# RWKV r, v and output weights split layers ahead and kept in DRAM, r and v in three products, bonus product on Pool

## The chip, the cores and the metric

One core of a Trainium2 chip runs the whole kernel. The metric is the device time in microseconds. The engines are TensorE (PE), VectorE (DVE), ScalarE (ACT), GpSimd (Pool) and SyncE (SP); SP issues nearly all DMAs. The 16 DMA engines of the core are shared by every transfer. On-chip memory is SBUF, and DRAM is the chip's own off-chip memory.

## The reference, cut to what matters

Two layers, SEQ = 256 tokens of D = 1024, float32. Layer 0 mixes by a gated MLP, layer 1 by RWKV-7; each layer has a SwiGLU FFN before and after the mixer and a gated embedding (ple) at its end.

```python
for i in range(DEPTH):                       # DEPTH = 2
    h = h + 0.5 * rms_norm(swiglu(rms_norm(h, g[0]), ffn_w13[i, 0], ffn_w2[i, 0]), g[1])
    m = gmlp_mixer(...) if i % 2 == 0 else rwkv7_mixer(...)
    h = h + rms_norm(m, g[3])
    h = h + 0.5 * rms_norm(swiglu(rms_norm(h, g[4]), ffn_w13[i, 1], ffn_w2[i, 1]), g[5])
    ...                                      # ple

# in rwkv7_mixer: H = 16 heads of N = 64
x_rkv = h[:, :, None, :] + dx[:, :, None, :] * mu[:3]
rkv = jnp.einsum('bsnd,nde->bsne', x_rkv, w_in)      # w_in[0], [1], [2]: r, k, v, 1024x1024 each
g = jax.nn.sigmoid(xg @ g1) @ g2
k = k * (1.0 + (a - 1.0) * k_a)
y = wkv7_scan(rh, heads(decay), kh, vh, -kk, kk * ah)
bonus = (jnp.sum(rh * kh * r_k, axis=-1, keepdims=True) * vh).reshape(B, S, D)
out = ((yn + bonus) * g) @ w_out                     # w_out: 1024x1024
```

## The kernel before, in words

The stages run in the order ffn00, gmlp, ffn01, ple0, ffn10, rwkv, ffn11, ple1, with seams in which the work of two neighbours is mixed. The Tile framework fixes the order of instructions on every engine when the program is built; an engine runs its own list strictly in order and waits on semaphores.

**Weights.** They come as units of 128x1024 float32 (512 KB). `emit_dma` has SP load a unit into one of 4 raw buffers (L134). `emit_split` casts it to fp32r on ACT, the high half (L154), and subtracts on DVE, the low half (L156); both halves go into one slot of 128x2048 (1 MB). There are 20 slots, handed out in a ring by `slot` and `drop`; weights and the activations of a stage share them. Four raw loads are issued ahead of the split, and `pump` splits at most 12 units ahead of their use. `mm3` multiplies split values in three fp32r products (L178 to L180). The FFN works by 11 chunks of 256 of the 2816 hidden columns: AT(c) multiplies by w13 (L400, which packs the products by one half), copies the result out (L408, ACT) and makes the gate; Dn(c) multiplies by w2 (L178 to L180).

**RWKV weights.** The k weights are split as usual. r (L1055) and v (L1307) are not: their "wf" loads of 1 MB (L146, two row blocks each) go into a slot, and both are multiplied in plain float32. The output weights (o) are split inside the stage, as slots come free.

**RWKV order.** `xprod(n)` makes the mixed input of projection n on DVE (L819). After k come the eight `r_step`s, among which `triangle` (L1039) makes the matrices that the scan inverts. A ladder of small DVE products and sums (L1091, L1093) then inverts the 16x16 diagonal blocks, and two transposes (L1094, L1095) hand the inverse to PE. While DVE climbs it, PE does `gate1` (L1171), the eight `v_step`s and `gate2` (L1198, L1203). `join(0)` (L1110) and `join(1)` (L1121) lie between the products of v_step(5) and v_step(6) and need the ladder's result. `inside(k)` (L1284, L1292) makes the scores of head pair k. Among the ladder DVE has eight products of r with the decay (L1268) and the bonus product kT*rT (L1269). Then `stack_v` (L1389) fills the state operands, and chunk(0) to chunk(3) run the recurrence, each as us (L1415), a copy (L1444), st (L1453) and y. `spread` (L1493) and `scaled` (L1504) normalise, `otr` transposes, and Dn(0), Dn(1) multiply by the output weights.

```python
        def r_step(k):
            w = self.need(at["r"] + k // 2)[0][:, k % 2]
            for m in range(KT):
                mm(psr[m // 2][:, (m % 2) * T:(m % 2 + 1) * T], lhsT=w[:, m * 128:(m + 1) * 128], rhs=xent(0, k),
                   start=k == 0 and m % 2 == 0, stop=k == KT - 1 and m % 2 == 1)
```

Of the kernel before, what the change touches and what calls it, by code (L numbers as in the profile page):

```python
# [60 lines left out]
class Trunk:  # L61
    NSLOT = 20

    def __init__(self, ctx, tc, io):
# [4 lines left out]
        ep = lambda name, bufs=1, **k: ctx.enter_context(tc.tile_pool(name=name, bufs=bufs, **k))
        self.slots = ep("slots")  # L70
        self.pp = ep("pp", space=bass.MemoryType.PSUM)
        self.rawp = ep("raw", 4)
# [17 lines left out]
        self.pq = {}  # L90

# [45 lines left out]
    def emit_split(self):  # L137
# [3 lines left out]
        if len(self.units[i]) > 3:  # L141
# [8 lines left out]
        src, p, n = self.units[i]  # L150
# [6 lines left out]
        self.hl[i] = (hl, hh, ll)  # L157
# [148 lines left out]
    def ffn_units(self, f):  # L306
# [468 lines left out]
    def rwkv_units(self):  # L775
# [6 lines left out]
        rows = lambda n: [(io["wrkv"][n, k * 256:(k + 1) * 256, :].rearrange("(k p) d -> p k d", p=128), 128, D, 2) for k in range(KT // 2)]  # L782
        put("k", [(io["wrkv"][1, k * 128:(k + 1) * 128, :], 128, D) for k in range(KT)])
        put("l", [(io["wl"], 128, 1024, 2)])
        put("r", rows(0))
        put("g1", [(io["g1"].rearrange("q p n -> p q n"), 128, 640, 2)])
        put("g2", [(io["g2"], 128, D, 2)])
        put("v", rows(2))
        put("o", [(io["bwout"][k * 128:(k + 1) * 128, :], 128, D) for k in range(KT)])
        return at  # L790

    def rwkv(self, at):
# [20 lines left out]
        def xprod(n, lo=0, hi=T, ks=range(KT)):  # L813
# [135 lines left out]
        xprod(0)  # L949
        wu_ = self.slot("wu")  # L950
# [100 lines left out]
        def r_step(k):  # L1051

            w = self.need(at["r"] + k // 2)[0][:, k % 2]
            for m in range(KT):
                mm(psr[m // 2][:, (m % 2) * T:(m % 2 + 1) * T], lhsT=w[:, m * 128:(m + 1) * 128], rhs=xent(0, k),  # L1055
                   start=k == 0 and m % 2 == 0, stop=k == KT - 1 and m % 2 == 1)
            if k % 2:
                self.release(at["r"] + k // 2)
# [210 lines left out]
        V.tensor_tensor(kT, kT, rT, op=ALU.mult)  # L1269
# [30 lines left out]
        def v_step(k, between=()):  # L1300

            x = xent(2, k)
            w = self.need(at["v"] + k // 2)[0][:, k % 2]
            between = list(between)
            for b in range(NB):
                for q in range(2):
                    mm(psv[b][q], lhsT=x[:, b * 128:(b + 1) * 128], rhs=w[:, q * 512:(q + 1) * 512], start=k == 0, stop=k == KT - 1)  # L1307
                    if between:
                        between.pop(0)()
            if k % 2:  # L1310
                self.release(at["v"] + k // 2)
                if k < 5:
                    P(1, 1)
# [27 lines left out]
        self.drop(X["x"][2])  # L1341
# [34 lines left out]

        sv = [self.slot("sv") for _ in range(2)]
        svv = [t.rearrange("p (c m h t) -> p c m h t", c=2, m=8, h=2) for t in sv]
        vv = vn.rearrange("p (b m h t) -> p b m h t", b=2, m=8, h=2)
        vm = self.small(32, "vm", 1)  # L1380
        vmv = vm.rearrange("p (b m h) -> p b m h", b=2, h=2)
        for b in range(NB):
            V.tensor_reduce(vm[:, b * 16:(b + 1) * 16], vn[:, b * D:(b + 1) * D].rearrange("p (h t) -> p h t", t=64), axis=AX.X, op=ALU.add)
            V.tensor_scalar(vm[:, b * 16:(b + 1) * 16], vm[:, b * 16:(b + 1) * 16], ck[:, 0:1], 1.0 / 64, op0=ALU.mult, op1=ALU.mult)

        def stack_v(c):
            rs = half[c % 2]
            for h in range(2):
                V.scalar_tensor_tensor(svv[c // 2][half[1 - h], c % 2, :, h, :], vv[rs, c // 2, :, h, :], ck[rs, 0:1],  # L1389
                                       vmv[rs, c // 2, :, h].unsqueeze(2).to_broadcast([64, 8, 64]), op0=ALU.mult, op1=ALU.subtract)  # L1390

        for c in range(NCH):
            stack_v(c)
        G.memset(svv[0][EV, 0, :, 0, :], 0.0)
        G.memset(svv[0][OD, 0, :, 1, :], 0.0)
# [284 lines left out]
```

## Time and profile before

| what | value |
|---|---|
| median of 3 runs | 1177.57 us (1177.08 to 1178.36) |
| the profiled execution's own time | 1183.38 us |
| its span | 1181.6 us |
| PE busy | 97% of the span |
| DVE, ACT, Pool busy | 73%, 56%, 6% |
| DMA, mean | 176 GB/s, 207.78 MB |
| ffn01's chunks 2 to 10 | 367.6 to about 510 us of the span |
| rwkv | about 741 to 957 us |

The span is that of the profiler's one execution; about 1.8 us lie around it. A busy PE is not PE at its fastest: the float32 products run longer for the same work, and in a few stretches the granted clock is below full. Times below are microseconds from the span's start.

### The profile page before, as it was taken

The numbers are of one execution on the slowest core, as the hardware profiler recorded it, in microseconds if no ns is written. First come the engines' busy times: TensorE is split into PE (matmuls) and PEld (weight loads), VectorE is DVE, ScalarE is ACT, GpSimd is POOL, SyncE is SP. The second block draws the span as 40 slices with busy tenths as digits, with TensorE's granted clock in tenths as the row PEclk, the third lists the DMA queues.
The fourth block names the chain that finished last, engine by engine and source line by source line (L and its number), as shares of the span: only waits on it lengthen the run. The fifth ranks groups of instructions, "written<-read, shape, count | busy, mean of one in ns | idle before, by whom it ended". The sixth has DMA issues, their size and how long they took to land. (4 is left out here: it accounts for less than half of the span.)

```text
span 1181.6 us, 18709 instructions
## 1 busy us (share of the span) xinstructions
PE 1151.2 (97%) x7284; PEld 954.3 (81%) x7284; DVE 859.1 (73%) x1299; ACT 659.7 (56%) x1145; POOL 72.5 (6%) x92
## 2 busy tenths in 40 slices
PE   8999999999999999999999999999998899999997
PEld 6788888888888888888888888777467778888886
DVE  5886666877678666667876666878859898676663
ACT  6665556545476555558755554374226396555553
POOL 0000000010010000001100000230000220000011
PEclk8999999999999999999999999999989999999999
DMA  7886654746586666646766664550300377666510
GB/s 244 292 295 196 190 172 152 253 156 205 186 271 202 194 192 184 192 134 196 248 189 194 193 192 144 178 183 1 125 4 21 108 249 263 193 189 193 177 47 36
DMA packets 58841, 207.78 MB, mean 176 GB/s; under 512 B 6784, under 2 KB 7296, under 8 KB 58496
## 3 DMA queue, kind: packets, MB, share of 16 engines
q1 hardware_dynamic: 58752, 206.59, 54.8%
q8 instruction: 57, 0.93, 0.3%
q14 instruction: 32, 0.26, 0.1%
HBM read 205.51 MB, written 1.05 MB: 175 GB/s over the span
## 5 line engine op out<-in xcount | busy, mean ns | idle before, releaser
L156 DVE TENSOR_TENSOR w<-raw,w 128x1024 fp32r<-128x1024 f32 x348 | 423.6, 1223 | 145.6 <-ACT w L154 139.8
L154 ACT CAST w<-raw 128x1024 fp32r<-128x1024 f32 x348 | 366.3, 1055 | 153.9 <-PE mm L400 68.7
L400 PE MATMUL mm<-xT,w 128*128 128x512 f32 (+1 forms) x2304 | 407.8, 337 | 0.0
L400 PEld LDWEIGHTS mm<-xT,w 128*128 128x128 f32 x2304 | 358.6, 189 | 50.0
L178 PE MATMUL acc<-w,hT 128*128 128x512 f32 x352 | 138.2, 393 | 0.0
L179 PE MATMUL acc<-w,hT 128*128 128x512 f32 x352 | 137.3, 390 | 0.0
L180 PE MATMUL acc<-w,hT 128*128 128x512 f32 x352 | 137.1, 389 | 0.0
L408 ACT COPY pn<-mm 128x256 f32<-128x256 f32 x144 | 46.6, 375 | 93.8 <-PE mm L400 93.8
L409 DVE TENSOR_TENSOR pn<-mm,pn 128x256 f32<-128x256 f32 x144 | 54.4, 418 | 39.3 <-ACT pn L408 39.3
L180 PEld LDWEIGHTS acc<-w,hT 128*128 128x128 f32 x352 | 66.1, 188 | 14.1
L178 PEld LDWEIGHTS acc<-w,hT 128*128 128x128 f32 x352 | 66.2, 188 | 12.6
L179 PEld LDWEIGHTS acc<-w,hT 128*128 128x128 f32 x352 | 66.3, 188 | 12.3
L232 POOL TENSOR_SCALAR rpost<-ss 128x1 f32<-128x1 f32 x15 | 7.5, 500 | 777.9 <-ACT junk L239 777.9
L178 PE MATMUL mm<-w,xT 128*128 128x512 f32 x128 | 51.8, 415 | 2.9 <-ACT w L154 2.6
L289 DVE SCALAR_TENSOR_TENSOR xT<-tr,gT,xT 128x128 fp32r<-128x128 f32 x112 | 35.6, 344 | 24.4 <-ACT xT L288 23.5
L179 PE MATMUL mm<-w,xT 128*128 128x512 f32 x128 | 51.4, 405 | 0.7 <-DVE xT L289 0.5
L412 DVE TENSOR_TENSOR pn<-pn,yc 128x512 f32<-128x512 f32 x72 | 49.7, 691 | 2.0
L180 PE MATMUL mm<-w,xT 128*128 128x512 f32 x128 | 50.9, 403 | 0.0
L179 PE MATMUL z<-w,xT 128*128 128x512 f32 x128 | 49.9, 390 | 0.0
L180 PE MATMUL z<-w,xT 128*128 128x512 f32 x128 | 49.9, 390 | 0.0
L178 PE MATMUL z<-w,xT 128*128 128x512 f32 x128 | 49.7, 393 | 0.0
L288 ACT ACTIVATE xT<-tr,gT 128x128 fp32r<-128x128 f32 x112 | 37.8, 371 | 19.3 <-PE tr L275 14.9
(282 smaller groups left out, 1534.8 us busy)
## 6 DMA issues: line engine op xcount, KB each, us to landing
raw<-in_w SPq DMA_DIRECT2D x264, 512.0 KB, 4.3
raw<-in_win SPq DMA_DIRECT2D x32, 512.0 KB, 4.4
raw<-in_wout SPq DMA_DIRECT2D x16, 512.0 KB, 4.8
raw<-in_wg SPq DMA_DIRECT2D x16, 512.0 KB, 3.9
wf<-in_wrkv SPq DMA_DIRECT2D x8, 1024.0 KB, 5.1
gbc<-in_norm_g SPq DMA_DIRECT2D x9, 512.0 KB, 5.4
raw<-in_wrkv SPq DMA_DIRECT2D x8, 512.0 KB, 3.5
raw<-in_bwout SPq DMA_DIRECT2D x8, 512.0 KB, 3.6
```

The lines of the kernel that those rows point to most:

```text
L154: self.high = self.nc.scalar.copy(hh, r[:p, :n])
L156: eng.tensor_tensor(ll, r[:p, :n], hh.bitcast(F32), op=ALU.subtract)
L178: mm(out, lhsT=lh, rhs=rh, start=start, stop=False)
L179: mm(out, lhsT=ll, rhs=rh, start=False, stop=False)
L180: mm(out, lhsT=lh, rhs=rl, start=False, stop=stop)
L232: nc.gpsimd.tensor_scalar(r, a, b, eps, op0=ALU.add, op1=ALU.add)
L288: done = (nc.scalar.activation(hi, v, AF.Copy, scale=gc), nc.vector.scalar_tensor_tensor(lo, v, gc, hi.bitcast(F32), op0=ALU.mult, op1=ALU ...
L289: nc.vector.scalar_tensor_tensor(lo, v, gc, hi.bitcast(F32), op0=ALU.mult, op1=ALU.subtract))
L400: nc.tensor.matmul(ps[i][:, :T] if s else ps[i], lhsT=w[:, sl], rhs=x, start=u + q + s == 0, stop=s + u == 2 and q == 3)
L408: nc.scalar.copy(zi, ps[i][:, T:])
L409: nc.vector.tensor_tensor(zi, ps[i][:, :T], zi, op=ALU.add)
L412: nc.vector.tensor_tensor(z2, z2, rbc.unsqueeze(1).to_broadcast([128, 2, T]), op=ALU.mult)
```

## The change

The r and v rows (16 units) join ffn01's list of units, two per chunk from c = 2 to 8 and one in c = 9 and 10; the o rows (8 units) join ffn10's, one per chunk from c = 2 to 9. They are split as every unit is, and `flush` then stores each slot to a DRAM tile (1 MB) and drops it. In the rwkv stage `emit_split` loads that tile (1 MB) into a slot. `parts` splits the inputs of r and v too: ACT casts the high half, and the low half comes from DVE and Pool (r) or Pool twice (v). `r_step` and `v_step` take three fp32r products. `xprod(5)` and `xprod(2)` move ahead of the ladder; kT*rT goes to Pool behind the last low half of v's input; mean and `stack_v` are spread between inside(4) and chunk(1).

```diff
     def emit_split(self):
...
+        self.flush()
+        if len(self.units[i]) > 4:
+
+            t = self.slot("w", F32R)
+            self.nc.sync.dma_start(t.bitcast(F32), self.parts.pop(self.units[i][3]))
+            self.hl[i] = (t, t[:, :1024], t[:, 1024:])
+            self.n_split += 1
+            return
...
+        if len(self.units[i]) > 3:
+
+            self.stores.append((self.units[i][3], hl))
+        else:
+            self.hl[i] = (hl, hh, ll)
...
+    def flush(self):
+        for key, hl in self.stores:
+            t = self.parts[key] = self.rdp.tile([128, 2048], F32, name=f"part_{key}", tag=f"part_{key}")
+            self.nc.sync.dma_start(t, hl.bitcast(F32))
+            self.drop(hl)
+        self.stores.clear()
...
             put(at13, c, w13(c))
             put(at2, c - 2, w2(c - 2))
+            for _ in range(-(-len(early) // (FC - c))):
+                key, src = early.popleft()
+                u.append((src, 128, 1024, key))
...
+        kept = lambda n: [(None, 128, D, f"{n}{k}", True) for k in range(KT)]
...
-        put("r", rows(0))
+        put("r", kept("r"))
...
-        put("v", rows(2))
-        put("o", [(io["bwout"][k * 128:(k + 1) * 128, :], 128, D) for k in range(KT)])
+        put("v", kept("v"))
+        put("o", kept("o"))
...
+        def parts(n, key, engs):
+
+            X[key] = [self.slot("xs", F32R) for _ in range(2)]
+            for i, e in enumerate(engs):
+                ks = slice(i * KT // len(engs), (i + 1) * KT // len(engs))
+                x, xh, xl = (g8(t)[:, ks] for t in (X["x"][n], *X[key]))
+                S.copy(xh, x)
+                L[key] = e.tensor_tensor(xl, x, xh.bitcast(F32), op=ALU.subtract)
+            self.drop(X["x"].pop(n))
...
         xprod(0)
+        parts(0, "r", (V, G))
+        P(1, 8)
...
+                mm(o, lhsT=wh[:, ms], rhs=xh, start=k == 0 and m % 2 == 0, stop=False)
+                mm(o, lhsT=wh[:, ms], rhs=xl, start=False, stop=False)
+                mm(o, lhsT=wl[:, ms], rhs=xh, start=False, stop=k == KT - 1 and m % 2 == 1)
...
+        xprod(5)
         P(1, 3)
-
+        xprod(2)
+        self.drop(hnT, dxT)
+        parts(2, "v", (G, G))
 
         nq = self.slot("nq")
...
-        xprod(5)
         gate1()
-        xprod(2)
-        self.drop(hnT, dxT)
...
-        V.tensor_tensor(kT, kT, rT, op=ALU.mult)
+        with behind("v"):
+            G.tensor_tensor(kT, kT, rT, op=ALU.mult)
...
+                    self.mm3(psv[b][q], xh, xl, wh[:, sl], wl[:, sl], k == 0, k == KT - 1)
...
+        mean_v(0)
+        stack_v(0)
...
         inside(4)
         inside(5)
+        stack_v(1)
...
         chunk(0)
         with behind("c"):
-            P(1, 0)
+            mean_v(1)
+            stack_v(2)
+            P(2, 1)
             vgain(0)
         chunk(1)
         with behind("c"):
-            P(1, 0)
+            stack_v(3)
+            P(2, 1)
             vgain(1)
...
+                    todo = [rows("r", self.io["wrkv"][0]) + rows("v", self.io["wrkv"][2]), rows("o", self.io["bwout"])]
+                    if dist < 2:
+                        early = todo[1 - dist]
+                plan.append(self.ffn_units(st[1] * 2 + st[2], early))
```

The order in which instructions stand shows three places. First SP's own queue in ffn01 (`raw<-in_w` loads an FFN unit, `raw<-in_wrkv` an r or v unit, `part_` is a DRAM tile). Before:

```order
L134 DMA raw<-in_w 128x1024 x18
L222 DMA gbc<-in_norm_g 128x1024
L134 DMA raw<-in_w 128x1024 x48
L134 DMA raw<-in_wp 128x1024 x2
L134 DMA raw<-in_wg 128x1024 x8
```

Of the change, the same place from its first store on:

```order
L181 DMA part_r_3282<-w_3238 128x2048
L138 DMA raw<-in_w 128x1024 x2
L138 DMA raw<-in_wrkv 128x1024 x2
L138 DMA raw<-in_w 128x1024 x3
L181 DMA part_r_3487<-w_3437 128x2048
L138 DMA raw<-in_w 128x1024
L181 DMA part_r_3505<-w_3489 128x2048
L138 DMA raw<-in_w 128x1024 x2
L138 DMA raw<-in_wrkv 128x1024 x2
L138 DMA raw<-in_w 128x1024 x3
```

Two 1 MB stores and two more 512 KB loads now stand among each chunk's loads, and the engines' split instructions with them.

Second, DVE where the ladder begins (`xr` is the mixed input, `wu` the inverse, `mx` the matrices). Before:

```order
L1259 TENSOR_TENSOR q_537_6885<-q_537_6885,kT_6925 128x2048
L1082 MEMSET wu_6881 128x32
L1083 STREAM_TRANSPOSE wu_6881<-mx_6996 128x1024
L1091 TENSOR_TENSOR pn<-wu_6881 128x2
L1093 TENSOR_REDUCE wu_6881<-pn 128x2
L1091 TENSOR_TENSOR pn<-wu_6881 128x8
L819 SCALAR_TENSOR_TENSOR xr_7250<-dxT_6588,chT,hnT_6587 128x256
```

Of the change:

```order
L1049 TENSOR_TENSOR bt_7171<-bt_7171,q_564_7061 128x1024
L846 SCALAR_TENSOR_TENSOR xr_7500<-dxT_6756,chT,hnT_6755 128x256 x7
L1126 MEMSET wu_7057 128x16
L1301 TENSOR_TENSOR q_564_7061<-q_564_7061,kT_7101 128x2048
L1127 MEMSET wu_7057 128x32
L1128 STREAM_TRANSPOSE wu_7057<-mx_7172 128x1024
L846 SCALAR_TENSOR_TENSOR xr_7511<-dxT_6756,chT,hnT_6755 128x256 x8
L1136 TENSOR_TENSOR pn<-wu_7057 128x2
L1138 TENSOR_REDUCE wu_7057<-pn 128x2
```

The eight pieces of xprod(5) moved to the other side of the first transpose, and those of xprod(2) from between the ladder's steps to ahead of them.

Third, Pool at the same place (`nq` is cleared for join(0), `xs` are the halves of v's input). Before:

```order
L904 TENSOR_TENSOR kn_6906<-kn_6906,gn_6907 128x1024
L1078 MEMSET nq_7192 128x2048
L1330 MEMSET xx_7385 32x32x32 x2
L1394 MEMSET sv_8079 64x8x64
L1395 MEMSET sv_8079 64x8x64
```

Of the change:

```order
L941 TENSOR_TENSOR kn_7082<-kn_7082,gn_7083 128x1024
L1123 MEMSET nq_7526 128x2048
L855 TENSOR_TENSOR xs_7521<-xr_7511,xs_7520 128x1024 x2
L1312 TENSOR_TENSOR kT_7101<-kT_7101,rT_7579 128x2048
L1372 MEMSET xx_7736 32x32x32 x2
```

Three products with two inputs each came between the two clears.

## Rows read from the trace of the kernel before

**Rows 1.** The page's head, and its DMA issue line of the unsplit loads.

```profile
span 1181.6 us, 18709 instructions
...
wf<-in_wrkv SPq DMA_DIRECT2D x8, 1024.0 KB, 5.1
```

**Rows 2.** Windows: length, busy time (instructions) of PE, PEld, DVE, ACT, POOL; clock; DMA share; GB/s.

```profile
60.00:80.00 20.00, 20.00 (x108) 17.30 (x107) 16.09 (x23) 13.19 (x20) 1.07 (x1) 1.00 0.91 308
384.60:500.00 115.40, 115.40 (x613) 99.62 (x612) 80.43 (x112) 61.59 (x97) 0.00 (x0) 1.00 0.62 189
820.20:849.10 28.90, 28.88 (x94) 14.56 (x94) 28.58 (x55) 9.38 (x18) 1.89 (x2) 1.00 0.27 92
849.10:871.00 21.90, 19.94 (x595) 11.43 (x597) 6.57 (x8) 0.59 (x1) 0.00 (x0) 0.77 0.16 52
```

**Rows 3.** Waits from 20 to 95 us: total, times, longest.

```profile
ACT w L154 <- DMA raw<-in_w: 16.7, 18, 2.8
```

**Rows 4.** Groups by form, 640 to 960 us: count, busy us, mean ns, idle before.

```profile
L156 DVE TENSOR_TENSOR w<-raw,w 128x1024 fp32r<-128x1024 f32 x48 | 58.2, 1221 | 17.2 <-ACT w L154 16.6
L154 ACT CAST w<-raw 128x1024 fp32r<-128x1024 f32 x48 | 50.4, 1053 | 19.7 <-PE mm L400 11.7 <-PE st L1453 3.0 <-PE acc L180 2.7
```

**Rows 5.** PE's timeline in ffn10: start, duration, engine, operation.

```profile
700.00 11.31 PE L400 MATMUL mm<-xT,w 128*128 128x512 f32 x64
711.15 0.40 PE L178 MATMUL acc<-w,hT 128*128 128x512 f32 x1
...
713.89 0.62 PE L400 MATMUL mm<-xT,w 128*128 128x512 f32 x2
```

**Rows 6.** PE's timeline in the rwkv stage.

```profile
785.54 14.08 PE L1055 MATMUL r<-xr,wf 128*128 128x256 f32 x64
...
820.22 4.58 PE L1171 MATMUL g<-wf,xr 128*128 128x160 f32 x32 [2.37 <-ACT rT L1250]
824.64 3.60 PE L1307 MATMUL v<-wf,xr 128*128 128x512 f32 x8
828.07 0.60 PE L1187 MATMUL g<-ident,gl 128*128 128x128 f32 x4
...
849.14 0.73 PE L1110 MATMUL q<-wu,nq 16*32 16x16 f32 x64
...
859.77 2.07 PE L1307 MATMUL v<-wf,xr 128*128 128x512 f32 x2
861.77 1.05 PE L1121 MATMUL x<-mx,nq 32*32 32x16 f32 x64
...
898.33 0.42 PE L1415 MATMUL us<-sv,sk 128*64 128x64 f32 x4 [2.70 <-DVE sv L1389]
...
904.09 1.15 PE L1453 MATMUL st<-sv,bn 128*64 128x64 f32 x28 [0.71 <-DVE sv L1444]
```

**Rows 7.** DVE's timeline in the rwkv stage.

```profile
811.29 2.29 DVE L1259 TENSOR_TENSOR q<-q,kT 128x2048 f32<-128x2048 f32 x1
...
817.18 1.94 DVE L1083 STREAM_TRANSPOSE wu<-mx 128x1024 f32<-128x1024 f32 x1 [3.54 <-ACT mx L1046]
...
838.52 2.28 DVE L1269 TENSOR_TENSOR kT<-kT,rT 128x2048 f32<-128x2048 f32 x1
...
843.97 2.12 DVE L1094 STREAM_TRANSPOSE wu<-wu 128x1024 f32<-128x1024 f32 x1
...
897.44 6.14 DVE L1389 SCALAR_TENSOR_TENSOR sv<-vn,ck,vm 64x512 f32<-64x512 f32 x8
```

**Rows 8.** Pool's timeline in the rwkv stage.

```profile
773.29 1.90 POOL L904 TENSOR_TENSOR kn<-kn,gn 128x1024 f32<-128x1024 f32 x1
...
911.08 0.32 POOL L1493 TENSOR_SCALAR gv<-gv,ck 128x8 f32<-128x8 f32 x1 [28.75 <-DVE gv L1492]
...
935.65 2.27 POOL L1493 TENSOR_SCALAR gv<-gv,ck 128x8 f32<-128x8 f32 x1 [2.63 <-DVE gv L1492]
```

**Rows 9.** DVE's timeline beside that last Pool row.

```profile
935.47 2.35 DVE L156 TENSOR_TENSOR w<-raw,w 128x1024 fp32r<-128x1024 f32 x2
```

More of the change, by code (lines that the diff above doesn't have):

```diff
@@ L90, in __init__ @@
         self.pq = {}
+        self.parts = {}
+        self.stores = []
     def slot(self, name, dt=F32):
@@ L129, in emit_dma @@
         self.n_dma += 1
-        if len(self.units[i]) > 3:
+        if len(self.units[i]) > 4:
             return
-        src, p, n = self.units[i]
+        if len(self.units[i]) > 3 and not isinstance(self.units[i][3], str):
+            return
+        src, p, n = self.units[i][:3]
         t = self.rawp.tile([128, 1024], F32, name="raw", tag="raw")
@@ L140, in emit_split @@
             self.emit_dma()
-        if len(self.units[i]) > 3:
+        self.flush()
+        if len(self.units[i]) > 4:
+            t = self.slot("w", F32R)
+            self.nc.sync.dma_start(t.bitcast(F32), self.parts.pop(self.units[i][3]))
+            self.hl[i] = (t, t[:, :1024], t[:, 1024:])
+            self.n_split += 1
+            return
+        if len(self.units[i]) > 3 and not isinstance(self.units[i][3], str):
             src, p, n, k = self.units[i]
@@ L149, in emit_split @@
             return
-        src, p, n = self.units[i]
+        src, p, n = self.units[i][:3]
         hl = self.slot("w", F32R)
@@ L1051, in r_step @@
         def r_step(k):
-            w = self.need(at["r"] + k // 2)[0][:, k % 2]
+            wh, wl = self.need(at["r"] + k)
+            xh, xl = (g8(t)[:, k] for t in X["r"])
             for m in range(KT):
[L1055 to L1058, printed above, removed]
+                o, ms = psr[m // 2][:, (m % 2) * T:(m % 2 + 1) * T], slice(m * 128, (m + 1) * 128)
+                mm(o, lhsT=wh[:, ms], rhs=xh, start=k == 0 and m % 2 == 0, stop=False)
+                mm(o, lhsT=wh[:, ms], rhs=xl, start=False, stop=False)
+                mm(o, lhsT=wl[:, ms], rhs=xh, start=False, stop=k == KT - 1 and m % 2 == 1)
+            self.release(at["r"] + k)
+            if k < 7:
                 P(1, 1)
@@ L1340, in rwkv @@
         v_step(7, join(2))
-        self.drop(X["x"][2])
+        self.drop(*X["v"])
         vn = self.slot("vn")
@@ L1346, in rwkv, with mean_v, stack_v @@
         self.unbank(*psv[0], *psv[1])
+        sv = [self.slot("sv") for _ in range(2)]
+        svv = [t.rearrange("p (c m h t) -> p c m h t", c=2, m=8, h=2) for t in sv]
+        vv = vn.rearrange("p (b m h t) -> p b m h t", b=2, m=8, h=2)
+        vm = self.small(32, "vm", 1)
+        vmv = vm.rearrange("p (b m h) -> p b m h", b=2, h=2)
+        def mean_v(b):
+            V.tensor_reduce(vm[:, b * 16:(b + 1) * 16], vn[:, b * D:(b + 1) * D].rearrange("p (h t) -> p h t", t=64), axis=AX.X, op=ALU.add)
+            V.tensor_scalar(vm[:, b * 16:(b + 1) * 16], vm[:, b * 16:(b + 1) * 16], ck[:, 0:1], 1.0 / 64, op0=ALU.mult, op1=ALU.mult)
+        def stack_v(c):
+            rs = half[c % 2]
+            for h in range(2):
+                V.scalar_tensor_tensor(svv[c // 2][half[1 - h], c % 2, :, h, :], vv[rs, c // 2, :, h, :], ck[rs, 0:1],
+                                       vmv[rs, c // 2, :, h].unsqueeze(2).to_broadcast([64, 8, 64]), op0=ALU.mult, op1=ALU.subtract)
+        mean_v(0)
+        stack_v(0)
+        G.memset(svv[0][EV, 0, :, 0, :], 0.0)
+        G.memset(svv[0][OD, 0, :, 1, :], 0.0)
         inside(4)
         inside(5)
+        stack_v(1)
         bn = [self.slot("bn") for _ in range(2)]
@@ L1375, in rwkv @@
         self.drop(bt, kt)
[L1377 to L1395, printed above, removed]
         yo = self.slot("yo")
@@ L1572, in run @@
             if st[0] == "ffn":
-                plan.append(self.ffn_units(st[1] * 2 + st[2]))
+                early = []
+                after = names[i + 1:]
+                if "rwkv" in after:
+                    dist = after[:after.index("rwkv")].count("ffn")
+                    rows = lambda n, w: [(f"{n}{k}", w[k * 128:(k + 1) * 128, :]) for k in range(KT)]
+                    todo = [rows("r", self.io["wrkv"][0]) + rows("v", self.io["wrkv"][2]), rows("o", self.io["bwout"])]
+                    if dist < 2:
+                        early = todo[1 - dist]
+                plan.append(self.ffn_units(st[1] * 2 + st[2], early))
             elif st[0] == "ple":
```

20 lines of the change are left out of this document (8 added, 12 removed).

## The prediction

> **What bounds the kernel now.** I read the windows first, then the timelines of the rwkv stage. In the FFNs PE never stops: from 384.6 to 500 us it is busy for all of the 115.4 us, DVE for 80.43, ACT for 61.59, and the DMA engines for 0.62 of the time at 189 GB/s [rows 2]. An FFN chunk uses six units of 524,288 bytes, so 189 GB/s make a chunk 16.6 us. Nothing that is added there to DVE, ACT or the DMAs costs time until it outgrows this slack. In the rwkv stage the bounds change every 20 to 30 us. From 820.2 to 849.1 PE is full (28.88 of 28.9) and DVE nearly so (28.58); from 849.1 to 871 PE is busy, DVE is not (6.57), and the granted clock averages 0.77 [rows 2]: part of this stretch ran at the lower level, 1.2 GHz. Then DVE leads: PE waits 2.70 us for the first state operand and 0.71 for a copy that stands behind all eight [rows 6].
>
> I predict the difference by segments, against the profiled execution. Its span is 1181.6 us [rows 1] and its own time 1183.38; the median of the runs is 1177.57, and I apply the difference to the median.
>
> **The FFNs.** ffn01 gains 16 splits at 1.05 us of ACT and 1.22 us of DVE [rows 4]: 16.8 us and 19.5 us in nine chunks (150 us). Over 115.4 us DVE had 35 us free and ACT 54 [rows 2], so PE covers them. The transfers are less safe. Between the first copies of chunk 2 and chunk 10, ACT's order has 55 casts where it had 46; the list would ask for 8 units a chunk, and the difference comes out of the lead, which shrinks by seven units. So 55 loads (28.8 MB) and 15 stores of 1 MB (15.7 MB) fall in 8 chunks of 16.6 us: 44.5 MB in 133 us, 335 GB/s. No stretch of before asks for that much over that long. The nearest is 60 to 80 us, 308 GB/s at a share of 0.91 [rows 2], which at a share of 1 would be 338. There ACT already waits for its loads, 16.7 us in 75 [rows 3], and PE is still busy for all of 60 to 80 [rows 2]: ACT's waits use up its slack first. So the demand stands at the edge. Bounds: 0, if the mixture of loads and stores gets 335 or more, and 133 x (335/308 - 1) = 12 us, if it gets 308. I take **+1.5**, nearer the first, since 308 came with a share below 1. ffn10 gets one unit a chunk: 7 loads and a store, 4.7 MB in 16.6 us or 284 GB/s, below that 308; I take 0.
>
> The Trainium skill, "DMA: Bandwidth & Descriptors", section "Specifications", gives about 358 GB/s as the limit of a core towards HBM; no run here shows that figure. By it the term would be 0.
>
> **r.** r took 14.08 us for 64 float32 matmuls, which are 32 (k, m) pairs: 0.44 us each [rows 6]. An fp32r product goes by pitch. From 711.15 to 713.89 twelve of 512 columns pass, 0.228 each; from 700.00 to 711.15 go 32 of 512 and 32 of 256 columns, which leaves 0.12 for 256 [rows 5]. Three are 0.36 instead of 0.44, so 64 pairs save 4.8 us. But PE has no use for it: the second triangle needs bt, the product ahead of DVE's row at 811.29 [rows 7], and one piece of xprod(5) now stands before it: 811.7. PE only waits longer there. DVE's pieces of xprod(5) fill the 3.54 us for which it waits ahead of the transpose at 817.18 [rows 7], and gate1 can start before 820.22. The first v product needs ACT's casts and Pool's low half of v's input behind xprod(2), which ends near 822; with a Pool product of 1.90 us [rows 8] that is about 824.1, where 824.64 stood [rows 6]. I take **-0.3** (bounds -3, +2).
>
> **v up to join(0).** v in float32: eight matmuls, four (k, b, q) products, from 824.64 to 828.07 [rows 6], 0.86 each; three fp32r products are 0.68. Steps 0 to 4 are 20 of them: 3.5 us. What would be late next is the inverse or a v load. The ladder loses the bonus product (2.28 us [rows 7]) and one split (1.22 [rows 4]), and the xprod pieces that stood in it are partly moved into the wait; its transpose, which started at 843.97 and took 2.12 [rows 7], ends at about 841.4. The loads of v2 to v7 wait for slots: v2's for ta, which ACT's copies let go, v3's for rT, which DVE's eight products and now Pool's 2 x 1.90 us bonus product [rows 8] let go. I estimate 830 and 834 for these, from the order of the copies and the product's 3.8 us behind 826; a 1 MB load lands after 5.1 us [rows 1], so near 835 and 839, just as PE comes to them. join(0) then stands at about 845.3 to 846.6 instead of 849.14 [rows 6]; I take **-2.5** (bounds -3.8 and the rival below).
>
> **v5 to v7.** In step 5, four products save 0.18 each: **-0.5** after the waits between. In step 6 the clock is low: two float32 matmuls, one product, run 861.77 - 859.77 = 2.0 us [rows 6]. Three fp32r products at half speed are 3 x 0.427 = 1.28 (I estimate 0.427 from 0.228 with its fill), four products: some -2.9 at most; the first of them need not be at the low clock, so **-1.7**. Step 7: **-0.7**.
>
> **The chunks.** The us products need the mean, its scaling and the first two stack_v products in either order, so the 2.70 us wait stays. The copy behind all eight (6.14 us [rows 7]) now has fewer ahead: st(0), which started at 904.09 after its wait [rows 6], starts some 2 us earlier. But mean(1) and stack_v(2), 1.2 + 0.2 + 1.5 us, now stand behind chunk 0's last DVE product, ahead of chunk 1's copies: +1.7. Eight splits, 9.8 us of DVE, are gone from the recurrence and the output; they lay mostly beside PE work. I take **-0.3** (bounds -3, +2.5). The o loads wait for slots alone, and need 5.1 us each; the first four can be there before Dn(0).
>
> **Sum:** 1.5 - 0.3 - 2.5 - 0.5 - 1.7 - 0.7 - 0.3 = -4.5 us. 1177.57 - 4.5 = **1173.1 us** (1178.9 by the profile's own time).
>
> **The rivals.**
>
> *Pool and DVE shut each other out (0.30).* The Pool addition took 0.32 us alone and 2.27 beside DVE's two-input subtractions, and ended when these did [rows 8, 9]. So Pool waits for DVE. Whether DVE waits for a Pool product no row shows. In the change, two low halves and the bonus product, 4 x 1.90 = 7.6 us, meet the ladder. If DVE waits for each, the inverse comes about 6.7 us later (a sum that stands between two products still runs, some 0.9 us in all): 848.1, and the v3 load, which needs the bonus product's end, at about 844 in place of 839. join(0) then falls at about 850.4, +1.2 in place of -2.5. The sum is -0.8: **1176.8**, no change. The Trainium skill, "SBUF — State Buffer", section "Who interferes with whom", says just this: a DVE instruction with two SBUF inputs and a GpSimd instruction that reads SBUF exclude each other for a whole instruction, and whoever issues first wins. The rows agree for Pool's side.
>
> *The DMA engines can't carry ffn01 (0.20), the slower side.* Place: chunks 2 to 9, raw loads late, ACT waits, and its copies out of PSUM come late for PE. At 308 GB/s the term is +12 in place of +1.5, the sum +6: **1183.6**. It decides the sign when the term passes 6 us, at 335/(1 + 6/133) = 321 GB/s. Against it: PE showed no wait in 60 to 80 with ACT waiting.
>
> *No low clock at v_step(6) (0.10).* The drop follows a stretch in which PE waited and ran small products. If these come with fewer waits and the clock stays at 2.4 GHz, join(1), at 1.05 us a piece [rows 6], goes too, and the whole segment is some 5 us shorter than the sum has it: **1168**.
>
> *No effect beyond noise (in the first rival's chance):* the saved PE time of r and v is only waited away; that is r's term, and would be v's if the v loads came 3 us later than I reckon.
>
> **How the numbers follow.** Main case 0.40, lock 0.30, DMAs 0.20, clock 0.10. A measurement of this kernel can tell about 2.4 us (0.2%) from no change. Faster: most of the main case (0.36), the clock case (0.10) and the part of the lock case in which DVE waits for only some of the products (0.09): 0.55. Same: 0.04 + 0.16 + 0.01 = 0.21. Slower: 0.05 of the lock case, and 0.19 of the DMAs' case: 0.24. Range: the low end is the clock case with some margin, 1166; the high end takes in the DMAs' case at 308 GB/s, 1184.5; a slower one stays outside. The likeliest case's own range is 1168 to 1176.
>
> **What would show it.** DMAs near 335 GB/s in ffn01 with PE still full; a few ACT waits for raw there. If PE shows gaps in AT chunks, the second rival holds. The r products end near 808 and PE waits for DVE until about 811.7. Pool's bonus product at 3.8 us, and the ladder's products no longer than before, or, by the first rival, single ladder products stretched to 2 us or more. q of join(0) near 845 to 847. v products 0.68 apart. The wait before st(0) gone, and a new one in chunk 1. Wrong it would be if the loads or stores stop PE, or if another wait of the rwkv stage takes the 3 to 4 us before join(0).

## The result, and the profile after

The change makes the kernel slower: 1193.67 us median of 4 runs (1191.72 to 1195.73) against 1177.96 (1177.08 to 1178.74), a ratio of 1.0126 [1.0109, 1.0144] as recorded (the two medians alone give 1.0133). 1173.1 was forecast, 1166 to 1184.5 as the range. The profiled execution took 1191.86 us, 8.5 more than that of before; a second profile of before (e1) took 1181.9. So the traces, read against each other, account for 8.5 to 10 of the 15.7 us between the medians; the rest is taken up below.

The page after, its head, four engines, and the new DMA issues:

```profile
span 1189.7 us, 19030 instructions
...
PE 1147.2 (96%) x7380; PEld 963.8 (81%) x7380; DVE 883.9 (74%) x1315; ACT 676.5 (57%) x1165; POOL 84.7 (7%) x96
...
raw<-in_w SPq DMA_DIRECT2D x264, 512.0 KB, 4.6
...
part_r<-w SPq DMA_DIRECT2D x8, 1024.0 KB, 7.9
part_v<-w SPq DMA_DIRECT2D x8, 1024.0 KB, 8.2
```

PE is busy for 4 us less in all (1147.2 against 1151.2), and yet the span is 8.1 us longer [rows 1]: PE waits more. Windows after, columns as in [rows 2]: ffn01's chunks, its end with the start of ple0, the wait for pT, the ladder, the stretch of v_step(6) and join(1), and the recurrence.

```profile
369.00:502.00 133.00, 133.00 (x711) 114.95 (x710) 100.17 (x138) 78.47 (x122) 0.00 (x0) 1.00 0.88 324
502.00:530.00 28.00, 26.22 (x125) 21.17 (x123) 23.22 (x31) 19.38 (x34) 2.86 (x4) 1.00 0.85 298
528.00:536.00 8.00, 4.21 (x15) 3.06 (x14) 7.50 (x16) 7.64 (x17) 0.86 (x2) 0.89 0.75 253
824.00:860.00 36.00, 29.42 (x144) 20.78 (x147) 33.96 (x50) 11.99 (x22) 13.23 (x6) 0.91 0.41 163
860.00:880.00 20.00, 18.29 (x659) 13.30 (x646) 10.64 (x13) 3.05 (x4) 1.05 (x2) 1.00 0.21 79
905.00:940.00 35.00, 30.50 (x684) 26.57 (x682) 26.17 (x54) 15.55 (x43) 5.52 (x6) 0.95 0.45 160
```

For the second of these places, before:

```profile
502.00:530.00 28.00, 28.00 (x140) 23.51 (x139) 18.26 (x27) 15.30 (x32) 1.72 (x4) 1.00 0.40 125
```

ffn01's chunks run at 324 GB/s with PE full for all of 133 us. Time goes at three places: behind ffn01, in the ladder (PE 29.42 of 36, where it was full [rows 2]), and in the recurrence. One place gains: 860 to 880 runs at the full clock, where 849.1 to 871 had 0.77 [rows 2]. ACT's waits in the chunks show that the DMA edge was near; they did not reach PE:

```profile
ACT w L166 <- DMA raw<-in_w: 33.6, 27, 2.7
```

What is late behind ffn01 are the splits that the chunks did not get to. From the end of ffn01's last AT product to the cast of pT, the input of ple0, ACT has 12 casts after and 4 before (windows with ACT's split casts alone: length, busy time (count), clock, DMA share, GB/s; after, then before):

```profile
507.70:532.50 24.80, 12.49 (x12) 1.00 0.84 297
...
509.50:528.10 18.60, 4.23 (x4) 1.00 0.32 106
```

That the longer list uses up the lead, so that its extra splits fall behind the last chunk, is called the lead theory below. SP's queue behind ffn01 (start, length, operation):

```profile
508.57 15.84 SPq L138 DMA_DIRECT2D raw<-in_wg  x8
525.50 1.90 SPq L138 DMA_DIRECT2D raw<-in_w  x2
528.91 0.33 SPq L512 DMA_DIRECT2D raw<-in_pT  x1
```

and PE's timeline after, its waits in brackets:

```profile
533.26 1.30 PE L201 MATMUL pp<-w,pT 128*128 128x512 f32 x4 [3.79 <-ACT pT L513]
...
817.60 3.58 PE L1078 MATMUL m<-kk,bt 64*64 64x64 f32 x64 [2.78 <-DVE bt L1049]
830.37 0.50 PE L201 MATMUL v<-w,xs 128*128 128x512 f32 x1 [1.79 <-ACT rT L1295]
851.98 0.79 PE L201 MATMUL v<-w,xs 128*128 128x512 f32 x1 [4.77 <-DMA w<-part_v]
...
909.65 0.33 PE L1497 MATMUL st<-sv,bn 128*64 128x64 f32 x2 [1.35 <-ACT sv L1487]
...
919.65 1.15 PE L1497 MATMUL st<-sv,bn 128*64 128x64 f32 x28 [1.05 <-DVE sv L1488]
929.16 1.17 PE L1497 MATMUL st<-sv,bn 128*64 128x64 f32 x28 [1.59 <-DVE sv L1488]
942.11 0.50 PE L202 MATMUL o<-w,oT 128*128 128x512 f32 x1 [2.31 <-DVE oT L302]
```

The ladder after, on DVE and then on Pool:

```profile
828.55 2.31 DVE L1136 TENSOR_TENSOR pn<-wu 128x2 f32<-128x2 f32 x1
...
831.09 2.11 DVE L1136 TENSOR_TENSOR pn<-wu 128x8 f32<-128x8 f32 x1
...
833.43 4.34 DVE L1136 TENSOR_TENSOR pn<-wu 128x18 f32<-128x18 f32 x1
...
838.01 0.22 DVE L1136 TENSOR_TENSOR pn<-wu 128x32 f32<-128x32 f32 x1
...
846.35 0.69 DVE L1310 TENSOR_TENSOR sk<-rT,tw 64x512 f32<-64x512 f32 x1
...
854.12 2.17 DVE L1139 STREAM_TRANSPOSE wu<-wu 128x1024 f32<-128x1024 f32 x1
```

```profile
828.21 4.97 POOL L855 TENSOR_TENSOR xs<-xr,xs 128x1024 fp32r<-128x1024 f32 x2 [2.22 <-ACT xs L854]
833.14 4.59 POOL L1312 TENSOR_TENSOR kT<-kT,rT 128x2048 f32<-128x2048 f32 x1
```

A product of 2 columns takes 2.31 us, one of 18 columns 4.34; each ends as a Pool product ends, and the first one behind them is back at 0.22. That such DVE products wait for Pool's is called the lock theory below. The load for which PE waits 4.77 us was issued right behind the last of DVE's eight products with the decay (846.35 and 0.69 long), and not behind Pool's bonus product, which ended at 837.73. SP, where it is the first of five:

```profile
847.10 2.47 SPq L149 DMA_DIRECT2D w<-part_v  x5
```

Measured from gMLP's first product, as later shifts are too, against e1: the seam to ffn10 costs 8.0 us, q of join(0) comes 13.3 late, v_step(7)'s end 6.6, the first us 8.5, the first output product 10.4, the end 10.1.

### The profile page after: what moved, and what is told of

Same layout as the page of the kernel before. It is cut to its first block, busy times and chain, and to the rows that moved or that the text cites. A ratio compares the mean times of both kernels' runs of the same rounds, so it can differ in the third digit from the quotient of the medians.

```text
span 1189.7 us, 19030 instructions
## 1 busy us (share of the span) xinstructions
PE 1147.2 (96%) x7380; PEld 963.8 (81%) x7380; DVE 883.9 (74%) x1315; ACT 676.5 (57%) x1165; POOL 84.7 (7%) x96
## 4 chain that ended last, share of the span: by engine, by line
PE 69%; DVE 13%; DMA 9%; ACT 5%; issue 3%; POOL 1%; SPq 0%; POOLq 0%; DVEq 0%; ACTq 0%
PE mm L427 25%; DMA raw<-in_w 7%; PE acc L202 6%; PE acc L201 6%; PE acc L203 6%; DVE w L168 3%; PE z L202 2%; PE z L201 2%; PE z L203 2%; PE mm L202 2%; PE mm L203 2%; PE mm L201 2%; ACT w L166 2%; PE tr L298 1%; DMA raw<-in_wrkv 1%
## 5 line engine op out<-in xcount | busy, mean ns | idle before, releaser
L168 DVE TENSOR_TENSOR w<-raw,w 128x1024 fp32r<-128x1024 f32 x364 | 442.0, 1223 | 144.8 <-ACT w L166 140.8
L166 ACT CAST w<-raw 128x1024 fp32r<-128x1024 f32 x364 | 381.2, 1054 | 169.3 <-DMA raw<-in_w 84.7
L201 PEld LDWEIGHTS acc<-w,hT 128*128 128x128 f32 x352 | 66.2, 188 | 13.5 <-ACT hT L443 0.9
L202 PE MATMUL z<-w,xT 128*128 128x512 f32 x128 | 50.0, 390 | 0.0
L440 ACT ACTIVATE k<-pn 128x256 f32<-128x256 f32 x72 | 30.1, 417 | 34.8 <-DVE pn L439 34.8
L203 PE MATMUL z<-w,xT 128*128 128x512 f32 x128 | 49.9, 390 | 0.0
```

The costliest lines, as they stand in the source:

```text
L166: self.high = self.nc.scalar.copy(hh, r[:p, :n])
L168: eng.tensor_tensor(ll, r[:p, :n], hh.bitcast(F32), op=ALU.subtract)
L201: mm(out, lhsT=lh, rhs=rh, start=start, stop=False)
L202: mm(out, lhsT=ll, rhs=rh, start=False, stop=False)
L203: mm(out, lhsT=lh, rhs=rl, start=False, stop=stop)
L440: nc.scalar.activation(sg, z[:, :T], AF.Silu)
```

## The experiments

Ratios are to before, from runs beside it, with 95% intervals; they are the record's, and the ratio of the two medians differs from them by up to 0.0012. The cuts of edits show the lines that matter, those of e2 to e8 against the change, the later ones against before.

**e1: the kernel before once more** (no edit).

> The kernel before once more, for a second profile. The change's profile stands 8.3 us above that of before, while the medians stand 15.7 us apart. If the profile of before was the odd one, this one takes 1177 to 1179 us, and its ffn00 runs like that of the change, whose gmlp begins 2.3 us earlier than in the profile of before. If not, it takes about 1183 us again and the change lost nothing there.

1181.9 us in its one, profiled, execution, where timed runs took 1176 to 1181. Its gMLP began 1.9 us earlier than in the first profile. So the first profile was odd in ffn00 alone; both profiles have the 10.2 us stretch at 1.2 GHz from about 859.

**e2: the early splits and stores, with the rwkv stage of before.** The stored tiles are not read; all of rwkv's order is that of before.

```diff
-        put("r", kept("r"))
+        put("r", rows(0))
-        put("v", kept("v"))
+        put("v", rows(2))
-        put("o", kept("o"))
+        put("o", [(io["bwout"][k * 128:(k + 1) * 128, :], 128, D) for k in range(KT)])
```

> The rwkv stage of before, with the early splits and stores of the change in ffn01 and ffn10; nothing reads what is stored. Lead theory: ffn01's list grows by more than its splits do, the lead is used up, and ple0's weights and pT come late: PE waits 3 to 4 us before the first pp product, the stretch from ffn01's last chunk to ffn10 is 6 to 8 us longer, then nothing; 1184 to 1186 us. Rival, that the rwkv stage alone loses the time: within 2 us of before, 1176 to 1180 us. Rival, that the DMA load costs throughout: a loss in each AT chunk of ffn01, 12 us or more.

1185.96 us, 1.0069 [1.0044, 1.0095]: as the lead theory has it. Its profiled execution took 1190.11.

```profile
534.83 2.07 PE L201 MATMUL pp<-w,pT 128*128 128x512 f32 x4 [4.18 <-ACT pT L513]
```

No chunk of ffn01 is longer; ffn10 begins 9.1 us late in this trace. By the medians some 7 us of the loss lie in the FFNs, with the rwkv stage's order untouched.

**e3: Pool's three products on DVE.**

```diff
-        parts(2, "v", (G, G))
+        parts(2, "v", (V, V))
-            G.tensor_tensor(kT, kT, rT, op=ALU.mult)
+        V.tensor_tensor(kT, kT, rT, op=ALU.mult)
```

> The change, with the low halves of v's input and the bonus product on DVE in place of Pool: 1.2 + 1.2 + 2.3 = 4.7 us more work for DVE and none for Pool. Lock theory: DVE's first three ladder products, 2.3, 2.1 and 4.3 us in the change, are back at 0.2, the inverse comes about 3.5 us earlier, and the kernel takes 1.5 to 4 us less than the change, 1190 to 1192 us. Rival, that the ladder was late through its loads or its inputs: the inverse comes 4 to 5 us later still, and the kernel takes as long as the change or 2 to 5 us longer.

1190.33 us, 1.0103 [1.0082, 1.0123]. DVE's ladder:

```profile
829.01 0.15 DVE L1136 TENSOR_TENSOR pn<-wu 128x2 f32<-128x2 f32 x1
...
836.84 2.28 DVE L1311 TENSOR_TENSOR kT<-kT,rT 128x2048 f32<-128x2048 f32 x1
...
850.25 2.23 DVE L1139 STREAM_TRANSPOSE wu<-wu 128x1024 f32<-128x1024 f32 x1
```

With 4.7 us more work DVE reaches the transpose 4.6 us earlier, 0.7 of which is a shorter seam, and all four runs are below those of the change. The lock theory holds.

**e4: mean and stack_v in one piece, as before.**

```diff
-        mean_v(0)
-        stack_v(0)
...
-        stack_v(1)
...
         self.drop(bt, kt)
+        mean_v(0)
+        mean_v(1)
+        for c in range(NCH):
+            stack_v(c)
...
-            mean_v(1)
-            stack_v(2)
...
-            stack_v(3)
```

> The change, with mean and stack_v in one piece ahead of chunk 0 as they stood before. If the new place behind chunks 0 and 1 costs what the trace suggests (the stretch from the first us product to the first output product is 1.9 us longer than before), the kernel takes 1 to 2 us less than the change, and us(0) comes later by what st(0) gains. Rival, that the place is neutral and the recurrence is long for another reason (slots, o loads): within 1 us of the change, 1193 to 1195 us.

1192.98 us, 1.0124 [1.0104, 1.0143]: 0.7 less than the change, which is within the spread. The stretch from us(0) to the first output product is 3.1 us shorter, but us(0) comes 0.7 later and the output products take 1.6 longer, with a piece at 1.2 GHz.

**e5: 8 units in each FFN** (r as before, v in ffn01, o in ffn10).

```diff
-                    todo = [rows("r", self.io["wrkv"][0]) + rows("v", self.io["wrkv"][2]), rows("o", self.io["bwout"])]
+                    todo = [rows("v", self.io["wrkv"][2]), rows("o", self.io["bwout"])]
...
-        put("r", kept("r"))
+        put("r", [(io["wrkv"][0, j * 256:(j + 1) * 256, :].rearrange("(k p) d -> p k d", p=128), 128, D, 2) for j in range(KT // 2)])
...
-        parts(0, "r", (V, G))
```

> The change with r left as it was before (unsplit, plain float32, loaded in the rwkv stage); v takes r's place in ffn01 (8 units, one per chunk) and o stays in ffn10. All else of the change stands. Lead theory (16 more splits than the pumps make have to be caught up between ffn01's last chunk and ple0): with 8 the stretch from there to ffn10 is at most 2 us longer than before in place of 7 to 8, and the kernel takes 5 to 7 us less than the change, 1186 to 1189 us. Rival, that each stored unit costs, wherever it stands: half of the loss stays, 1189 to 1191 us. r in float32 should cost nothing, since PE waits for bt there.

1194.6 us, 1.0125 [1.0108, 1.0141]: the sum was missed, the seam not.

```profile
369.00:502.00 133.00, 133.00 (x711) 114.94 (x710) 99.00 (x139) 77.68 (x121) 0.00 (x0) 1.00 0.81 280
502.00:530.00 28.00, 28.00 (x139) 23.41 (x138) 18.39 (x28) 15.59 (x33) 1.72 (x4) 1.00 0.42 129
...
845.85 0.79 PE L201 MATMUL v<-w,xs 128*128 128x512 f32 x1 [4.17 <-DMA w<-part_v]
...
862.00:883.00 21.00, 20.39 (x398) 15.01 (x397) 7.07 (x10) 3.04 (x4) 1.05 (x2) 0.52 0.08 28
```

PE is full behind ffn01 and ffn10 begins 0.8 us late in place of 8.0. ACT has 4 casts between the last AT product and pT, as before. The rwkv stage then lost 11.5 us: q is late by Pool and the v load as in the change, and behind it 21 us run at a mean clock of 0.52, where the change had 1.00.

**e6: pT ahead of the raw loads**, in a slot of its own.

```diff
+            if c == 7 and filler is not None:
+                self.pr[l] = self.slot("pr")
+                nc.sync.dma_start(self.pr[l][:, :512], self.io["pT"][l])
```

> The change, with pT loaded into a slot of its own at chunk 7 of ffn01, ahead of the raw loads it stands behind in SP's queue. If pT in that queue is what PE waits for, the 3.8 us wait before the first pp product goes, and with it a stretch at 1.2 GHz: 4 to 6 us less than the change, 1188 to 1190 us. Rival, that the splits of ple0's weights are late as well: the wait moves to the wp or wg products and the kernel takes 0 to 2 us less, 1192 to 1194 us.

1195.14 us, 1.0131 [1.0115, 1.0146]: the rival. The 3.8 us wait is gone; PE waits 2.4 us for ffn01's last hT (the gated columns that Dn multiplies) instead, and 6.8 us at 1.2 GHz follow. Not pT alone but the splits due there are late; which of their parts, the loads, ACT's casts or DVE's differences, sets the time was not tried.

**e7: two more pumps per chunk in ffn01, one in ffn10.**

```diff
-            AT(c); P(1)
+            AT(c); P(1 + self.more.get(l * 2 + j, 0))
```

> The change, with two more pumps per chunk in ffn01 and one in ffn10, so that the list's extra units are asked for in the chunk they stand in, and not forced by their use. ACT's order has 193 casts ahead of chunk 10's first copy as before it, since the scheduler places them by its own times, and 210 ahead of pT in place of 207. Lead theory as the order has it: the catching up stays, and three more casts stand ahead of pT: within 2 us of the change, 1192 to 1196 us. Rival, that the forced splits make PE wait: 3 to 7 us less than the change.

1198.0 us, 1.0156 [1.0141, 1.0171], 2 us above what was expected. ACT has 210 casts ahead of pT in place of 207, and PE waits 6.27 us at the first gate product for DVE's transposed input. That the three more casts push this input back is argued, not shown. To ask earlier did not help here.

**e8: e5 with e3, e4, one more pump per chunk**, and the last scaled() held behind the first transposed output.

```diff
-            with behind("c"):
+            with behind("c", *(["tv"] if c == 3 else [])):
```

> r as before; v in ffn01 and o in ffn10, 8 units each, with one more pump per chunk; low halves of v's input and bonus product on DVE; mean and stack_v in one piece as before; and the last normalising products held behind the low half of the first transposed output, for which Dn(0) waits 2.3 us in the change. If the three losses found add up (seam 7 to 8, Pool 3 to 4, operands and Dn(0) 2 to 3 us), what is left is the gain of v in three products and of the splits taken out of the stage: 2 to 5 us less than before, 1173 to 1177 us. Rival, that the gain itself is not there, since the ladder and not v sets join(0): as before, 1177 to 1180 us.

1190.55 us, 1.0091 [1.0061, 1.0121]: missed. The seam cost 4.5 us again, 17 us ran at 1.2 GHz from 862.6, ffn11 lost 4 us, with raw loads that began at 957 in place of 928 in e1, and Dn(0) still waited 1.86.

**e9 to e12: one part alone on the kernel before.** e9 takes v (as in e5, on DVE), e10 the bonus product on Pool, e11 the spread operands, e12 o. Edits of e10 and e12 (e11's is e4's the other way round):

```diff
-        V.tensor_tensor(kT, kT, rT, op=ALU.mult)
+        G.tensor_tensor(kT, kT, rT, op=ALU.mult)
...
-        put("o", [(io["bwout"][k * 128:(k + 1) * 128, :], 128, D) for k in range(KT)])
+        put("o", [(None, 128, D, f"o{k}", True) for k in range(KT)])
...
+                    todo = [[], rows("o", self.io["bwout"])]
```

> Of the change only v: its 8 units split in ffn01 (one per chunk) and kept, three products, its input's low halves and the bonus product on DVE, xprod(5) and xprod(2) ahead of the ladder. r, o and the state operands as before. If the gain that was forecast for v is there once its costs are gone, the stretch from the first r product to the end of v_step(7) is 2 to 5 us shorter than before and the kernel takes 1174 to 1178 us. Rival, late loads: a kept v step needs a 1 MB load of its own where two steps shared one, slots come free late, PE waits 2 to 4 us for the load of v3 and falls to 1.2 GHz after it: 1180 to 1186 us.

> Before, with the bonus product alone moved from DVE to Pool. Lock theory: one ladder product of DVE waits for Pool's 3.8 to 4.6 us, more than the 2.3 us that DVE is spared; the inverse comes about 2 us later, join(0) too, and the kernel takes 0.5 to 2.5 us more than before, 1179 to 1181 us. Rival, no lock: DVE is spared 2.3 us, PE sets join(0) there, 0 to 1 us less than before.

> Before, with mean and stack_v alone spread as in the change (the first two ahead, the last two behind chunks 0 and 1). If the place costs, the waits before st in chunks 1 and 2 appear as in the change, us(0) to o(0) is 1 to 2.5 us longer than before, and the kernel takes 1 to 2.5 us more. Rival, that in the change the tail was long because of the o loads: no difference, within 1 us of before.

> Before, with the output weights alone split in ffn10 (one per chunk), kept and loaded in the rwkv stage. The seam of ffn01 is untouched: no difference up to rwkv. Without the splits between its products DVE's order puts the low half of the first transposed output behind a wait for Pool: Dn(0) waits 2 us in place of 0.7. If that and the later raw loads of ffn11 are all, the kernel takes 1 to 3 us more than before; if the 9.8 us of splits taken out of the recurrence count, 1 to 3 us less.

| part | median us | ratio |
|---|---|---|
| e9 v | 1184.65 | 1.0046 [1.0027, 1.0064] |
| e10 bonus on Pool | 1183.69 | 1.0046 [1.0028, 1.0063] |
| e11 operands | 1182.64 | 1.0040 [1.0027, 1.0053] |
| e12 o | 1176.92 | 0.9991 [0.9980, 1.0002] |

e10, DVE, Pool and PE:

```profile
818.72 4.65 DVE L819 SCALAR_TENSOR_TENSOR xr<-dxT,chT,hnT 128x256 f32<-128x256 f32 x1
...
818.44 4.65 POOL L1269 TENSOR_TENSOR kT<-kT,rT 128x2048 f32<-128x2048 f32 x1 [18.34 <-ACT rT L1250]
...
823.42 6.34 PE L1171 MATMUL g<-wf,xr 128*128 128x160 f32 x28 [3.81 <-DVE xr L819]
```

The lock alone: a DVE product of 0.48 us takes 4.65, as long as Pool's. It struck xprod(5), so gate1 waited and v began 6.7 us late; the kernel took 5.0 us more, where 0.5 to 2.5 was expected. In e11 the wait before st in chunk 1 is 2.00 us, and us(0) to the first output product takes 4.1 us longer than in e1; the kernel took 4.0 us more, where 1 to 2.5 was expected. e12 shows the wait of Dn(0), 1.88, and gains elsewhere what this costs. In e9 the rival's price came, not its mechanism: PE waited 0.65 and 0.84 us for v loads, q was 0.6 us earlier than before, and then 17 us went at the low clock:

```profile
860.00:875.00 15.00, 15.00 (x341) 10.24 (x339) 5.29 (x7) 2.46 (x3) 1.05 (x2) 0.56 0.01 3
```

**e13: e8 without extra pumps and without the forced order. e14: r alone on the kernel before**; the edit is e14's.

```diff
-        put("r", rows(0))
+        put("r", [(None, 128, D, f"r{k}", True) for k in range(KT)])
...
+                    todo = [rows("r", self.io["wrkv"][0]), []]
...
+        parts(0, "r", (V, G))
```

> e8 without the extra pumps and without the order forced on the last normalising products: r as before, v in ffn01 and o in ffn10 with 8 units each, low halves and bonus product on DVE, operands in one piece. If e8 lost its time through the extra pumps (seam of ffn01 5 us, and late raw loads in ffn11), the seam is at most 1.5 us longer than before, and the kernel takes what v alone and o alone add up to, 1180 to 1184 us. Rival, that v and o kept together disturb each other (slots, the order of the loads): 1187 us or more.

> Before, with r alone split in ffn01 (8 units, one per chunk), kept, loaded as eight tiles of 1 MB, and multiplied in three products; its input's low half on DVE and Pool. If r's saved PE time is only waited away, PE waits 2 to 3 us more before the second triangle, the first gate product comes no earlier, and the kernel is within 1.5 us of before, 1177 to 1180 us. Rival, that the eight extra loads or the Pool half delay k's last transposes or the first r product: 2 to 4 us more than before.

e13: 1184.06 us, 1.0041 [1.0020, 1.0061]; ffn10 began 0.1 us from before's place, so the extra pumps had cost e8 its seam. v and o don't disturb each other. In its trace 850 to 876 ran at a mean clock of 0.61.

The record has the mean granted clock of every run, and within e8, e9 and e13 the time goes by it:

| kernel | runs at the higher mean clock, us | runs at the lower, us |
|---|---|---|
| e8 | 0.989 to 0.990: 1184.58 to 1187.51 (3) | 0.980 to 0.982: 1193.58 to 1195.41 (3) |
| e9 | 0.989 to 0.994: 1178.99 to 1184.01 (6) | 0.983 to 0.987: 1185.29 to 1188.00 (6) |
| e13 | 0.988 to 0.993: 1175.83 to 1181.51 (3) | 0.982 to 0.984: 1183.24 to 1185.84 (6) |

By these means one and the same kernel ran with and without the long stretch at 1.2 GHz, and most of what v seems to cost is that stretch: e13's two runs at 0.991 and more, 1178.73 and 1175.83 us, are about level with before's median of 1177.82. e10 and e11 cost some 4 us at such a clock too: at 0.991 and more they took 1180.90 to 1184.66 us, against 1178.66 for before.

e14: 1176.15 us, 0.9982 [0.9969, 0.9995], a little faster. Its trace has PE waiting 2.53 us before the second triangle, as forecast for r, but the first gate product comes 3.5 us sooner after r's start, and the 2.37 us wait for the copies of r [rows 6] is gone.

**e15: r and o together** (the first line). **e16: e15 with xprod(5) ahead of the ladder**, behind r_step(7).

```diff
+                    todo = [rows("r", self.io["wrkv"][0]), rows("o", self.io["bwout"])]
...
+        xprod(5)
-        xprod(5)
         gate1()
```

> r and o of the change together, 8 units each in ffn01 and ffn10, with v, the bonus product and the operands as before. If the parts add, the kernel takes 2 to 4 us less than before, 1174 to 1177 us, and is the fastest of the study. Rival, that o's later raw loads of ffn11 or the two together cost what they bring: within 1.5 us of before.

> e15 with xprod(5) ahead of the ladder as in the change, in DVE's wait for the first transpose. The first gate product comes about 2.4 us earlier, as it did wherever this was done, and PE, which is full until join(0), keeps most of it: 1 to 2.5 us less than e15. Rival, that the ladder now sets join(0) or that PE waits there in small pieces and falls to 1.2 GHz: as e15 or 1 to 3 us more.

e15: 1174.6 us, 0.9958 [0.9944, 0.9971]; e16: 1175.87, 0.9969 [0.9955, 0.9982]. r and o together beat both kernels; o alone can't be told from no change. xprod(5)'s place adds nothing that can be told, where 1 to 2.5 us were expected. In e15's profile the stretch behind q keeps the full clock:

```profile
835.00:876.00 41.00, 39.50 (x842) 22.41 (x841) 26.89 (x33) 7.13 (x12) 2.86 (x4) 1.00 0.17 60
```

## Why the prediction was wrong, point by point

Against e1 the segments came to +8.0 us (the FFNs, forecast +1.5), +0.4 (r, -0.3), +4.9 (v up to join(0), -2.5), -6.7 (v5 to v7, -2.9) and +3.8 (the chunks, -0.3). Three terms had the wrong price or sign, and the one that erred the other way owed it to the clock.

**FFNs, +1.5: the first step that failed.** The demand was priced rightly for ffn01's chunks, and even high: 324 GB/s, PE full, no loss; the second rival did not come, though ACT waited 33.6 us. But the prediction noted that seven units come out of the lead and priced the demand only while the lead lasts. The 16 splits all stand ahead of pT, 8 of them between the last AT product and pT (12 casts in place of 4), where PE has too little to cover them: +8.0 us. The prediction had no term for this place. e2 shows this with the old rwkv stage, e5 and e13 that 8 units cost under 1 us there; e6 and e7 that neither pT's place nor earlier pumps mend it. That ffn10 itself loses nothing was right.

**r, -0.3.** The waits for bt came (0.97 and 2.78), so PE's saving in the triangles is waited away. But gate1 begins 1.7 us earlier than r's shift would have it, in e14 3.5: the term was too small. v began no earlier in the change, as forecast.

**v up to join(0), -2.5: the second step that failed; the first rival came instead**, at +4.9. DVE waits for Pool's streaming products as Pool waits for DVE [rows 8, 9]; e3 and e10 show it from both sides. The rival's chain held but for one link: the inverse is late (854.12), and the v load, for which PE waits 4.77 us, is held up by DVE's last product with the decay (ended 847.04, load issued 847.10), not by Pool's bonus product (ended 837.73). The rival was sized +1.2, since it counted neither the stretch of Pool's own products (4.97 and 4.59 in place of 3.8) nor that DVE's products with the decay, and with them the slots, come later too. The Trainium skill, "SBUF — State Buffer", section "Who interferes with whom", gave the rule; by these rows (2.31, 2.11, 4.34, 4.65 us) it held for whole instructions beside Pool's products over 1024 and 2048 columns, and 0.30 was too little for it.

**v5 to v7, -2.9.** From q to v_step(7)'s end the change gained 6.7 us. The price was too small because the stretch behind q ran at 2.4 GHz: here the rival without the low clock, which had 0.10, came. The term also took its gain from a low clock in the profile of before, which most timed runs seem to have lacked (below), and was then applied to their median. The 6.7 us are not v's merit: in e5, e8, e9 and e13, v in three products with r in float32, 17 to 20 us of it ran at 1.2 GHz. Each time PE waited 1.7 to 2.7 us at join(0)'s products, at its own issue, and the low clock followed; in e12 and e15 the wait was 0.35 and 1.50 and none did; in e14 it was 2.05 and 3.4 us at 1.2 GHz followed. That the wait decides it was not tried, and what decides how long the low clock stays is open.

**The chunks, -0.3.** The third step that failed: +3.8 came by the first output product. us(0) was 2 us later against v_step(7) rather than level. The wait before st(0) was to go, but 1.35 us for ACT's copy stand in place of 0.71 for DVE's; chunk 1 has the new wait of 1.05 that was named, and chunk 2's went from 1.14 to 1.59. e11 shows the cost of the spread by itself. That Dn(0) would wait 2.31 us for the low half of oT, behind a DVE product that waits for Pool, was not in the sum.

**What stays open.** The medians are 15.7 us apart, the profiles 8.5 (10.0 with e1). Both profiles of before hold 10.2 us at 1.2 GHz near 859, worth 5 us:

```profile
859.50:869.80 10.30, 10.30 (x212) 4.98 (x206) 1.70 (x3) 0.00 (x0) 0.00 (x0) 0.50 0.01 3
```

Their mean granted clock was 0.989. Of the 86 timed runs of before that stand beside the experiments 82 had 0.991 or more, most of them 0.993 or 0.994; the change's four had 0.985 to 0.988. A mean higher by 0.004 to 0.005 over 1180 us is what 10 us less at half the clock make (an estimate), so most timed runs of before seem to lack that stretch; with its 5 us the traces come to 13.5 to 15 of the 15.7. Where the low clock lay in a timed run no trace shows. What sets it is the main thing left open: it came and went between runs of one kernel.

## What to carry to other kernels

Work that is moved ahead into a list with a lead was paid here where the lead is refilled, not where it is listed: count what is due between the last covered instruction and the next stage, and spread it until nothing is. A long Pool product beside a chain of small two-input DVE products cost DVE Pool's whole duration, so moving it off a full DVE can lose more than it frees. And a change of many parts is best measured part by part: here r and o together gained 0.4%, the bonus product on Pool and the spread operands cost 0.4% to 0.5% each, v cost 0.5% by its median but little where the clock stayed up, and the place of the splits cost more than any. Put the mean granted clock beside each time, or a stretch at the low clock is taken for the cost of an edit.

## What was not expected of the hardware

A mixture of 512 KB loads and 1 MB stores held 324 GB/s for 133 us at a share of 0.88, above the 308 of [rows 2]; its fastest 30 us (415 to 445) came to 364 at 0.94. Pool's product of 128x2048 took 4.59 to 4.65 us beside DVE, where two of 1024 would take 3.8 alone. Not every Pool instruction holds DVE up: Pool's product of 128x16 took 3.21 us, and beside it four of xprod's products took 1.67 in all and a two-input subtraction its usual 1.22 (Pool, then DVE, in the change):

```profile
775.84 3.21 POOL L939 TENSOR_TENSOR gn<-gn,mhalf 128x16 f32<-128x16 f32 x1
...
775.41 1.67 DVE L846 SCALAR_TENSOR_TENSOR xr<-dxT,chT,hnT 128x256 f32<-128x256 f32 x4
777.00 1.22 DVE L855 TENSOR_TENSOR xs<-xr,xs 128x1024 fp32r<-128x1024 f32 x1
```

A stretch at 1.2 GHz behind join(0) cost as much as the parts under test, and of e13's nine runs three had a mean clock (0.988 to 0.993) above that of the other six (0.982 to 0.984), with the same kernel.
